# A Hymba layer on one core: the first raw conv weights loaded ahead of the stores of split weights, and the w_up pieces laid over the turned conv input

## The chip, the cores and the metric

One Trainium2 chip, one of its cores. The time is device microseconds of one launch of the whole layer, the median of three runs. Lower is better. The engines are PE (matrix products), DVE and ACT (vector and scalar work), POOL (GpSimd) and SP, which here only issues transfers; the transfers themselves are carried by the core's 16 DMA engines.

## The reference

One layer, on x of 1 x 2048 x 1024 in float32 (2048 positions, width 1024, 8 heads of 64 with 2 key/value heads, a causal window of 128, 512 conv channels, an MLP of 4096). Weights and gains are inputs.

```python
h = rms_norm(x, attn_norm_g)
z = h @ w_in                       # columns: q 512, k 128, v 128, gate_b 512, gate_c 512, xc 512
q, k = rms_norm(q, q_norm_g), rms_norm(k, k_norm_g)
y_attn = swa_sink_attention(q, k, v, sinks)
y_conv = gate_b * short_conv(gate_c * xc, conv_w)      # 3 taps, causal, per channel
y = concat([rms_norm(y_attn, attn_out_g), rms_norm(y_conv, conv_out_g)])
x = x + y @ w_out
hm = rms_norm(x, mlp_norm_g)
x = x + square(relu(hm @ w_up)) @ w_down
```

## The kernel before

**Arithmetic.** Each product of float32 matrices is made as three products of a high and a low part: ACT casts a raw tile to the high part, DVE subtracts it from the raw tile for the low part (this pair is called a split below). PE then multiplies high by high, high by low and low by high (L266 to L268, `mm3`). Weights are split once, in the first chunk, and both parts are stored to DRAM (`keep`, L223), so that later chunks load them ready-made (`weights`, L230, with c above 0).

**Stages.** The 2048 positions are worked in 4 chunks of 512 rows, each in 4 tiles of 128. Of the first chunk, the function `first_chunk` (L476) is ordered by hand: it loads x and the q columns of w_in in 8 pieces k, splits them (`split0`), turns x, scales it (`moved`), multiplies (`product0`, L508), and then does the k and v columns (qkv2, L266 to L268 into pz) and moves the results to z with ACT (L565 for q, L571 for k and v). At k of 3 it issues the raw load of qkv2 and, behind it, the small loads of conv taps and gains (`load_gains(1)`: cw, g_cols, g_y, L465 to L472). Then the mixers of the four chunks run: attention blocks (q and k normalised at L634 to L641, turned by PE at L652, scores at L679), between them the conv's products (pc from the weights wc, px from wx, pb from wb, in pairs of channel tiles j of 0 and 1, `conv_pair`), and the out projection (pout, from w_wo). Then MLP up (u, L1421), in a scheme of seven products p over blocks of 512 by 512 in place of eight, with wop as the split w_up and op_x as the split input; then MLP down (d, L1528).

**Order.** Outside the hand-ordered part a scheduler puts the work of every engine in an order by priorities. `ahead` raises them, and LATER (250) lowers them for the stores of split weights. Each engine runs its instructions in that order, and an instruction that waits holds up all behind it. SP issues the loads and most of the stores; it uses 8 semaphores in turn, so an issue also waits until the transfer eight issues before it has landed.

**Memory.** Tiles are taken from pools by tag; a tag has a number of buffers, used in turn, and a new tile waits until the readers of the old one in the same buffer are done. Raw weights share 2 buffers (tag "raw"), split weights 4 (tag "w", NW, 2 for each weight): w_wb takes the buffers of w_wc. The split w_q takes 4 buffers of "wop" and, for k of 4 to 7, buffers of "at" (`hl0`). Rows of x for the residual are in tag "x1" (4 buffers). When the mixers end, their pool is closed, and MLP up opens one in the same memory (L1094 on). There a memset of one element to the first tile of each tag (L1105) sets the order in which the tags are laid out, and so which old tile lies under which new one. Tag "w" there has 17 buffers for raw pieces of w_up (`wu`, loaded at L411), of 128 x 512.

Lines of the profile that the prediction uses: raw loads of weights L239, raw qkv L547, split stores of qkv2 and of each weight L228, stores of w_q L586, casts and subtractions of a split weight L245 and L246, x1 loads L965, xt_a loads L370; in MLP up the loads of w_up L411, their splits L416 and L417, op_x loads L396 and casts L397, the store of x to x_dram by POOL L913, its reload as xt_m for the last chunk's norm L1219, copies and activations of u by ACT L1176 and L1179.

Of the kernel before, what the change touches and what calls it, by code (L numbers as in the profile page):

```python
# [7 lines left out]
F32 = mybir.dt.float32  # L8
F32R = mybir.dt.float32r
# [7 lines left out]
P = 128  # L17
D = 1024
S = 2048
KD = D // P  # L20
# [82 lines left out]
def hymba_layer(  # L103
# [119 lines left out]
    def keep(hl, name):  # L223
        parts_dram[name] = [dram.tile([P, 2048], F32, name=f"{name}_{i}") for i in range(2)]

        with tc.high_priority(offset=-LATER):
            for d, t in zip(parts_dram[name], hl):
                nc.sync.dma_start(d, t.bitcast(F32))  # L228

    def weights(src_list, c, name, gains=(None,) * 4):  # L230

        if c:
            hl = high_low(c, f"w_{name}{c}")
            for d, t in zip(parts_dram[name], hl):
                nc.sync.dma_start(t.bitcast(F32), d)
            return hl
        raw = raw_part(f"raw_{name}")
        for dst, src in src_list(raw):
            nc.sync.dma_start(dst, src)  # L239
        hl = high_low(c, f"w_{name}")  # L240
        with ahead(7):
            for i, g in enumerate(gains):
                r = slice(i * 512, (i + 1) * 512)
                if g is None:
                    nc.scalar.copy(hl[0][:, r], raw[:, r])  # L245
                    nc.vector.tensor_tensor(hl[1][:, r], raw[:, r], hl[0][:, r].bitcast(F32), op=ALU.subtract)  # L246
                else:
                    nc.scalar.activation(hl[0][:, r], raw[:, r], AF.Copy, scale=g)
                    nc.vector.scalar_tensor_tensor(
                        hl[1][:, r], raw[:, r], g, hl[0][:, r].bitcast(F32), op0=ALU.mult, op1=ALU.subtract  # L250
                    )
        keep(hl, name)
        return hl
# [182 lines left out]
    z0 = [zrow(f"z0_{t}") for t in range(NT)]  # L436
    raw0 = [raw_part(f"raw_q{half}") for half in range(2)]
    hl0 = [wop_pool.tile([P, 2, AW], F32R, tag="wop", name=f"w_q0_{k}", bufs=NWOP) for k in range(NWOP)]
    hl0 += [pool.tile([P, 2, AW], F32R, tag="at", name=f"w_q0_{k}", bufs=NAT) for k in range(NWOP, KD)]
    h = parts(pool, "h", "a0")  # L440


# [15 lines left out]
    def load_gains(part):  # L458
        if not part:
            nc.sync.dma_start(g_qk[:, 0, :], q_norm_g[0].partition_broadcast(P))  # L460
            nc.sync.dma_start(g_qk[:, 1, :], k_norm_g[0].partition_broadcast(P))
            nc.sync.dma_start(sink, sinks[0].partition_broadcast(P))
            return
        for t in range(3):
            nc.sync.dma_start(cw[:, :, t], conv_w[0][t].rearrange("(i p) -> p i", p=P))  # L465
        nc.sync.dma_start(g_cols, mlp_norm_g[0].rearrange("(k p) -> p k", p=P))
        for kv in range(KVH):
            nc.sync.dma_start(
                g_y[kv * DH : (kv + 1) * DH, 0, :],
                attn_out_g[0][kv * GQ * DH : (kv + 1) * GQ * DH].rearrange("(i d) -> d i", d=DH),  # L470
            )
        nc.sync.dma_start(g_y[:, 1, :], conv_out_g[0].rearrange("(i p) -> p i", p=P))  # L472

    def first_chunk(first):

# [66 lines left out]
        for k in range(KD):  # L542
            split0(k)
            moved(k)
            if k == KH - 1:
                raw = raw_part("raw_qkv2")
                nc.sync.dma_start(*cols256(wi, AW)(raw)[0])  # L547
                load_gains(1)
            if k >= KH:
                norm_stats(x0[:, k - KH], f"a0_{k - KH}", rs0[:, k - KH : k - KH + 1])  # L550
            if k + 1 < KD:
                product0(k, [(i, t) for i in range(3) for t in range(NT)])
            else:
                product0(k, [(i, t) for t in range(NT) for i in range(3)])
            if k + 2 < KD:
                turn(k + 2)
        rs0_in = nc.gpsimd.tensor_tensor(rs0_2, rs0, rs0, op=ALU.mult).ins
        hl = high_low(0, "w_qkv2")
        for i in range(4):
            r = slice(i * 512, (i + 1) * 512)  # L560
            nc.scalar.copy(hl[0][:, r], raw[:, r])
            nc.vector.tensor_tensor(hl[1][:, r], raw[:, r], hl[0][:, r].bitcast(F32), op=ALU.subtract)
        w4 = [w.rearrange("p (k c) -> p k c", k=KD) for w in hl]
        for t in range(NT):
            nc.scalar.activation(z0[t][:, :AW], pzs[t], AF.Copy, scale=rs0[:, t : t + 1])  # L565
        for t in range(NT):
# [2 lines left out]
            for k in range(KD):  # L569
                mm3(ps, lambda s, k=k: hk(s, k), lambda s, k=k: w4[s][:, k, :], k == 0, k == KD - 1)  # L570
            z_in.append(nc.scalar.activation(z0[t][:, AW:], ps, AF.Copy, scale=rs0[:, t : t + 1]).ins)  # L571
        return rs0_in, hl

    z_in = []

    with tc.tile_pool(name="first", bufs=1) as first:
        with tc.manual_schedule(engines={ET.PE, ET.Activation, ET.DVE, ET.Pool, ET.SP}):
            rs0_in, w_qkv2 = first_chunk(first)

    keep(w_qkv2, "qkv2")  # L580
    for half in range(2):
        d = dram.tile([2, P, 2048], F32, name=f"q{half}")
        parts_dram[f"q{half}"] = [d[i] for i in range(2)]
        with tc.high_priority(offset=-LATER):
            for k in range(KH):
                nc.sync.dma_start(  # L586
                    d[:, :, k * AW : (k + 1) * AW].rearrange("i p c -> p i c"), hl0[half * KH + k].bitcast(F32)
                )

    with tc.tile_pool(name="mix_small", bufs=1) as mix_small, tc.tile_pool(name="mix", bufs=1) as mix:

# [199 lines left out]
        def conv_pair(c, h, j, yt, ssc):  # L793
# [30 lines left out]
            for i in range(2):  # L824
# [14 lines left out]
                conv.append(y)  # L839
                yield  # L840
            hl = weights(cols256(wi, O_B + j * 256), c, f"wb{j}")
            for i in range(2):
                ct = 2 * j + i
                ps = bank("mm", f"pb_{nm}_{i}")
                yield from group(hl, ps, i)
                y = conv[i]
                with ahead(10):
                    nc.vector.tensor_tensor(y, ps, y, op=ALU.mult)
                    yh = wop_pool.tile([P, 2, CH], F32R, tag="wop", name=f"yt_{nm}_{i}", bufs=NWOP)
                    yt.append(yh)  # L850
                    nc.scalar.copy(yh[:, 0], y)
                    nc.vector.tensor_tensor(yh[:, 1], y, yh[:, 0].bitcast(F32), op=ALU.subtract)
                    if ct == 0:
                        nc.scalar.activation(ssc, y, AF.Square)
                    else:
                        nc.scalar.activation(y, y, AF.Square)
                        nc.vector.tensor_tensor(ssc, ssc, y, op=ALU.add)
                yield
# [96 lines left out]
        def besides(c, before, h, yt, rc, x1, h_next, z_next):  # L955

            yield from before
            ssc = mix.tile([P, CH], F32, tag="ssc", name=f"ssc{c}", bufs=1)
            for j in range(2):
                yield from conv_pair(c, h, j, yt, ssc)  # L960
            for t in range(NT):
                r = (c * NT + t) * P
                xr = row("x1", f"x1_{c}_{t}", NT)
                with nullcontext() if c else tc.issue_after(z_in[-1]):
                    nc.sync.dma_start(xr, xf[r : r + P, :])  # L965
                x1.append(xr)
            out = out_projection(c, 1, yt, rc, x1)
            if c + 1 < NCHUNK:
                h_next += parts(pool, "h", f"h{c + 1}")
                steps = prepare(xf, (c + 1) * CH, g_row[0], h_next, f"a{c + 1}")  # L970
            else:
                steps = prepare_mlp(gain_row(mlp_norm_g, "g_mlp"))
            for i, _ in enumerate(steps):
                yield
                for j in range(STEPS):
                    next(out, None)
                    yield
                    if (i, j) == PC:
                        pc = bank("tr", f"pc{c}")
                        for t in range(NT):  # L980
                            nc.tensor.matmul(
                                pc[:, t : t + 1], ssc[:, t * P : (t + 1) * P], mean, start=True, stop=True
                            )
                        ms = mix_small.tile([P, NT], F32, tag="msc", name=f"ms_c{c}", bufs=1)

                        with tc.high_priority(offset=SOON):
                            if c:
                                nc.vector.tensor_copy(ms, pc[:, :NT])
                                rsqrt(rc, ms)
                            else:  # L990
                                nc.vector.tensor_tensor(ms, pc[:, :NT], rs0_2, op=ALU.mult)
                                rsqrt(rc, ms)
                                nc.gpsimd.tensor_tensor(rc, rc, rs0, op=ALU.mult)
            yield from out
            if c + 1 < NCHUNK:
                yield from project_qkv(c + 1, h_next, z_next)
            else:
                begin_mlp()
# [102 lines left out]
        return pool.tile([P, BW], F32, tag=tag, name=name, bufs=UP_BUFS[tag])  # L1101


    for tag in ("f12", "s1", "s2", "s4", "u4", "f11", "w"):
        nc.gpsimd.memset(piece(tag, f"{tag}_first")[:, :1], 0.0)  # L1105


    class Weights:
# [459 lines left out]
```

## Time and profile before

| what | us |
|---|---|
| median of 3 runs | 1934.71 (1933.54 to 1935.15) |
| the profiled execution | 1934.5 |
| its span, first to last instruction | 1932.8 |
| PE busy | 1913.2 |
| DVE busy | 1204.1 |
| ACT busy | 830.8 |
| POOL busy | 275.9 |
| PE busy in MLP up (L1421), 2688 products | 611.7 |
| PE busy in MLP down (L1528), 2688 products | 609.4 |
| DMA, mean over the span | 214 GB/s |

The span is what lies between the first and the last instruction; the 1.7 us beside it are start and end. Matmuls overlap in the array, so a group's "mean of one" (390 ns in MLP up) is longer than the spacing of two, and spacing is what counts. The granted clock of PE was 0.998 on the mean. Read a row of a timeline as: start, duration, engine, line, operation, what is written from what is read, shapes, how many; the bracket gives the idle time of the engine ahead of it and what ended it. SPq is SP's issue of a transfer; DMA in the chain of waits is from issue to landing.

### The profile page before, as it was taken

Reading aid. Unit: us, or ns where it says so; the run is one execution under the profiler, and the core shown is the slowest. Engines: PE = TensorE matmul, PEld = TensorE weight load, DVE = VectorE, ACT = ScalarE, POOL = GpSimd, SP = SyncE. Lnnn points to the kernel's source line nnn. Section 1 sums busy time; section 2 is a strip of 40 time slices with the busy share of each in tenths; the row PEclk is TensorE's granted clock in tenths of the full one; section 3 lists DMA queues with packets and bytes.
Section 4 is the critical chain, followed back from the end, with each engine's and each line's share of the span. In section 5 each row is a group of like instructions: output and inputs, shape, how many; then the busy total and the mean of one; then the engine's idle time right before and its main releaser. Section 6 shows DMA issues by size and latency. Waiting matters only on the chain.

```text
span 1932.8 us, 24559 instructions
## 1 busy us (share of the span) xinstructions
PE 1913.2 (99%) x8923; PEld 1589.5 (82%) x8923; DVE 1204.1 (62%) x1848; ACT 830.8 (43%) x1565; POOL 275.9 (14%) x474
## 2 busy tenths in 40 slices
PE   8999999999999989999999999999999999999999
PEld 7888888888888778888888888888888888888887
DVE  4886657447456768989877766766534334448541
ACT  5564435335344437444565554554422233232320
POOL 1122212302221112223201110101000000100000
PEclk9999999999999999999999999999999999999999
DMA  9884854464463888777665544537964457766631
GB/s 295 321 306 135 312 211 175 187 249 153 193 267 140 264 282 283 232 235 245 209 233 195 181 162 138 169 124 294 378 211 152 142 164 228 264 228 223 206 135 55
DMA packets 232792, 414.32 MB, mean 214 GB/s; under 512 B 51672, under 2 KB 136160, under 8 KB 219872
## 3 DMA queue, kind: packets, MB, share of 16 engines
q1 hardware_dynamic: 203840, 336.98, 51.8%
q0 software_dynamic: 15424, 51.40, 6.8%
q10 hardware_dynamic: 13408, 24.39, 3.3%
q8 instruction: 70, 1.15, 0.2%
q14 instruction: 50, 0.41, 0.1%
HBM read 286.87 MB, written 125.83 MB: 214 GB/s over the span
## 4 chain that ended last, share of the span: by engine, by line
PE 93%; DMA 2%; DVE 2%; issue 1%; POOL 1%; ACT 1%; SPq 0%; ACTq 0%; POOLq 0%; DVEq 0%
PE d L1528 32%; PE u L1421 31%; PE pout L266 2%; PE pout L268 2%; PE pout L267 2%; PE pz L266 2%; PE pz L267 2%; PE pz L268 2%; PE psc_b L679 2%; PE pc_c L266 2%; PE px_c L266 2%; PE px_c L267 2%; PE pc_c L267 2%; PE pc_c L268 2%; PE px_c L268 2%; PE pb_c L267 1%
## 5 line engine op out<-in xcount | busy, mean ns | idle before, releaser
L1421 PE MATMUL u<-op_x,wop 128*128 128x512 f32 x2688 | 611.7, 390 | 4.6 <-ACT wop L416 4.6
L1528 PE MATMUL d<-op_w,op_f 128*128 128x512 f32 x2688 | 609.4, 389 | 0.0
L1421 PEld LDWEIGHTS u<-op_x,wop 128*128 128x128 f32 x2688 | 505.4, 188 | 110.3 <-ACT wop L416 5.2
L1528 PEld LDWEIGHTS d<-op_w,op_f 128*128 128x128 f32 x2688 | 504.5, 188 | 104.8
L398 DVE TENSOR_TENSOR op_f<-op_f 128x1024 fp32r<-128x1024 f32 x112 | 136.9, 1225 | 234.0 <-ACT op_f L397 233.6
L397 ACT CAST op_f<-op_f 128x1024 fp32r<-128x1024 f32 x112 | 117.5, 1050 | 353.3 <-DMA op_f<-fop 350.2
L416 ACT CAST wop<-wu 128x512 fp32r<-128x512 f32 x156 | 96.2, 620 | 89.9 <-PE u L1421 82.4
L417 DVE TENSOR_TENSOR wop<-wu,wop 128x512 fp32r<-128x512 f32 x156 | 110.6, 710 | 32.6 <-ACT wop L416 17.3
L1157 POOL DMA_DIRECT2D fop<-s x96 | 52.2, 543 | 440.5 <-DVE s L1160 436.3
L1163 DVE TENSOR_TENSOR u<-u,u 128x512 f32<-128x512 f32 x128 | 87.7, 685 | 22.1 <-PE u L1421 22.0
L398 DVE TENSOR_TENSOR op_w<-raw,op_w 128x1024 fp32r<-128x1024 f32 x56 | 68.4, 1222 | 26.3 <-ACT op_w L397 26.2
L397 ACT CAST op_w<-raw 128x1024 fp32r<-128x1024 f32 x56 | 58.8, 1053 | 44.9 <-PE d L1528 22.6
L1169 ACT ACTIVATE u<-u 128x512 f32<-128x512 f32 x64 | 40.5, 632 | 62.9 <-DVE u L1163 61.0
L696 ACT ACTIVATE sc_b<-sc_b,ngm_b 128x128 f32<-128x128 f32 x128 | 49.6, 389 | 25.6 <-DVE ngm_b L693 25.6
L728 POOL TENSOR_SCALAR_AFFINE_SELECT pp_b<-pp_b 128x512 fp32r<-128x512 f32 x60 | 39.8, 675 | 112.8 <-ACT pp_b L721 59.2
L1370 POOL DMA_DIRECT2D wds<-raw x16 | 8.6, 536 | 328.1 <-DVE raw L1368 328.1
L416 ACT CAST wop<-wu_s 128x512 fp32r<-128x512 f32 x64 | 39.6, 620 | 32.2 <-PE u L1421 26.1
L417 DVE TENSOR_TENSOR wop<-wu_s,wop 128x512 fp32r<-128x512 f32 x64 | 45.0, 702 | 12.4 <-ACT wop L416 12.1
L266 PE MATMUL pout<-w_wo,yt_c 128*128 128x512 f32 x128 | 52.5, 410 | 0.0
L268 PE MATMUL pout<-w_wo,yt_c 128*128 128x512 f32 x128 | 52.1, 407 | 0.0
L267 PE MATMUL pout<-w_wo,yt_c 128*128 128x512 f32 x128 | 51.2, 400 | 0.0
L266 PE MATMUL pout<-w_wo,at_b 128*128 128x512 f32 x128 | 50.2, 395 | 0.0
(256 smaller groups left out, 3109.4 us busy)
## 6 DMA issues: line engine op xcount, KB each, us to landing
op_f<-fop SPq DMA_DIRECT2D x112, 512.0 KB, 4.3
raw<-in_w_down_dram SPq DMA_DIRECT2D x72, 512.0 KB, 4.3
wu<-in_w_up_dram SPq DMA_DIRECT2D x128, 256.0 KB, 4.1
w_wo<-wo SPq DMA_DIRECT2D x24, 1024.0 KB, 6.8
fop<-s POOLq DMA_DIRECT2D x96, 256.0 KB, 2.5
fop<-u ACTq DMA_DIRECT2D x64, 256.0 KB, 2.9
op_x<-xop SPq DMA_DIRECT2D x28, 512.0 KB, 6.4
w_q<-q SPq DMA_DIRECT2D x12, 1024.0 KB, 6.2
```

Of the source, the lines that this page charges most:

```text
L266: nc.tensor.matmul(ps, st(0), mv(0), start=first, stop=False)
L267: nc.tensor.matmul(ps, st(0), mv(1), start=False, stop=False)
L268: nc.tensor.matmul(ps, st(1), mv(0), start=False, stop=last)
L397: nc.scalar.copy(op[:, 0], raw)
L398: nc.vector.tensor_tensor(op[:, 1], raw, op[:, 0].bitcast(F32), op=ALU.subtract)
L416: splits.append(nc.scalar.copy(hi, blk).ins)
L417: nc.vector.tensor_tensor(lo, blk, hi.bitcast(F32), op=ALU.subtract)
L696: nc.scalar.activation(sc[:, hd, :], sc[:, hd, :], AF.Exp, bias=ngm[:, hd : hd + 1], accum_out=den[:, hd : hd + 1])
L1157: eng.dma_start(fop_dram[tb][ORDER_DOWN.index(i)][n // 2][:, n % 2], b)
L1163: return nc.vector.tensor_tensor(dst, ps, b, op=ALU.add).ins
L1421: nc.tensor.matmul(pt, wops[i][:, a, k, :], xops[tb, p][k // 2][:, b, k % 2, :], start=p not in GOES_ON and k + j == 0, stop=k + j == NB + ...
L1528: nc.tensor.matmul(ps[tb][j], fs[tb][:, a, k, j * P : (j + 1) * P], w[:, b, k, :], start=first and p not in GOES_ON and k + n == 0, stop=l ...
```

## The change

In the first chunk: the raw load of wc (the first pair of conv weights) moves from the scheduled part into `first_chunk`, at k of 7, and the small gain loads go behind it; the stores of qkv2 and of w_q 0 to 3 are issued at the end of `first_chunk`; the stores of w_q 4 to 7 are written behind the first wb weights, without the lowered priority; the split w_q 4 to 7 lie in rows of x1 in place of "at"; the loads of x for the residual of chunk 0 have no pinned predecessor. In MLP up: the memsets lay the tags out in another order, with two more (st, xt), and w last.

```diff
--- before.py
+++ after.py
@@ -227,6 +227,15 @@
             for d, t in zip(parts_dram[name], hl):
                 nc.sync.dma_start(d, t.bitcast(F32))
 
+    raws = {}
+
+    def load_raw(src_list, name):
+
+        raw = raw_part(f"raw_{name}")
+        for dst, src in src_list(raw):
+            nc.sync.dma_start(dst, src)
+        return raw
+
     def weights(src_list, c, name, gains=(None,) * 4):
 
         if c:
@@ -234,9 +243,7 @@
             for d, t in zip(parts_dram[name], hl):
                 nc.sync.dma_start(t.bitcast(F32), d)
             return hl
-        raw = raw_part(f"raw_{name}")
-        for dst, src in src_list(raw):
-            nc.sync.dma_start(dst, src)
+        raw = raws.pop(name, None) or load_raw(src_list, name)
         hl = high_low(c, f"w_{name}")
         with ahead(7):
             for i, g in enumerate(gains):
@@ -436,7 +443,7 @@
     z0 = [zrow(f"z0_{t}") for t in range(NT)]
     raw0 = [raw_part(f"raw_q{half}") for half in range(2)]
     hl0 = [wop_pool.tile([P, 2, AW], F32R, tag="wop", name=f"w_q0_{k}", bufs=NWOP) for k in range(NWOP)]
-    hl0 += [pool.tile([P, 2, AW], F32R, tag="at", name=f"w_q0_{k}", bufs=NAT) for k in range(NWOP, KD)]
+    hl0 += [row("x1", f"w_q0_{k}", NT, F32R).rearrange("p (i c) -> p i c", i=2) for k in range(NWOP, KD)]
     h = parts(pool, "h", "a0")
 
 
@@ -471,6 +478,14 @@
             )
         nc.sync.dma_start(g_y[:, 1, :], conv_out_g[0].rearrange("(i p) -> p i", p=P))
 
+    def keep_q(half):
+        d = dram.tile([2, P, 2048], F32, name=f"q{half}")
+        parts_dram[f"q{half}"] = [d[i] for i in range(2)]
+        for k in range(KH):
+            nc.sync.dma_start(
+                d[:, :, k * AW : (k + 1) * AW].rearrange("i p c -> p i c"), hl0[half * KH + k].bitcast(F32)
+            )
+
     def first_chunk(first):
 
         x0 = first.tile([P, NT, D], F32, name="x0")
@@ -543,8 +558,9 @@
             split0(k)
             moved(k)
             if k == KH - 1:
-                raw = raw_part("raw_qkv2")
-                nc.sync.dma_start(*cols256(wi, AW)(raw)[0])
+                raw = load_raw(cols256(wi, AW), "qkv2")
+            if k == KD - 1:
+                raws["wc0"] = load_raw(cols256(wi, O_C), "wc0")
                 load_gains(1)
             if k >= KH:
                 norm_stats(x0[:, k - KH], f"a0_{k - KH}", rs0[:, k - KH : k - KH + 1])
@@ -560,6 +576,8 @@
             r = slice(i * 512, (i + 1) * 512)
             nc.scalar.copy(hl[0][:, r], raw[:, r])
             nc.vector.tensor_tensor(hl[1][:, r], raw[:, r], hl[0][:, r].bitcast(F32), op=ALU.subtract)
+        keep(hl, "qkv2")
+        keep_q(0)
         w4 = [w.rearrange("p (k c) -> p k c", k=KD) for w in hl]
         for t in range(NT):
             nc.scalar.activation(z0[t][:, :AW], pzs[t], AF.Copy, scale=rs0[:, t : t + 1])
@@ -569,25 +587,13 @@
             for k in range(KD):
                 mm3(ps, lambda s, k=k: hk(s, k), lambda s, k=k: w4[s][:, k, :], k == 0, k == KD - 1)
             z_in.append(nc.scalar.activation(z0[t][:, AW:], ps, AF.Copy, scale=rs0[:, t : t + 1]).ins)
-        return rs0_in, hl
+        return rs0_in
 
     z_in = []
 
     with tc.tile_pool(name="first", bufs=1) as first:
         with tc.manual_schedule(engines={ET.PE, ET.Activation, ET.DVE, ET.Pool, ET.SP}):
-            rs0_in, w_qkv2 = first_chunk(first)
-
-    keep(w_qkv2, "qkv2")
-    for half in range(2):
-        d = dram.tile([2, P, 2048], F32, name=f"q{half}")
-        parts_dram[f"q{half}"] = [d[i] for i in range(2)]
-        with tc.high_priority(offset=-LATER):
-            for k in range(KH):
-                nc.sync.dma_start(
-                    d[:, :, k * AW : (k + 1) * AW].rearrange("i p c -> p i c"), hl0[half * KH + k].bitcast(F32)
-                )
-
-
+            rs0_in = first_chunk(first)
 
     with tc.tile_pool(name="mix_small", bufs=1) as mix_small, tc.tile_pool(name="mix", bufs=1) as mix:
 
@@ -839,6 +845,8 @@
                 conv.append(y)
                 yield
             hl = weights(cols256(wi, O_B + j * 256), c, f"wb{j}")
+            if not c and not j:
+                keep_q(1)
             for i in range(2):
                 ct = 2 * j + i
                 ps = bank("mm", f"pb_{nm}_{i}")
@@ -961,8 +969,7 @@
             for t in range(NT):
                 r = (c * NT + t) * P
                 xr = row("x1", f"x1_{c}_{t}", NT)
-                with nullcontext() if c else tc.issue_after(z_in[-1]):
-                    nc.sync.dma_start(xr, xf[r : r + P, :])
+                nc.sync.dma_start(xr, xf[r : r + P, :])
                 x1.append(xr)
             out = out_projection(c, 1, yt, rc, x1)
             if c + 1 < NCHUNK:
@@ -1101,8 +1108,10 @@
         return pool.tile([P, BW], F32, tag=tag, name=name, bufs=UP_BUFS[tag])
 
 
-    for tag in ("f12", "s1", "s2", "s4", "u4", "f11", "w"):
+    for tag in ("u2", "f11", "f12", "s1", "s2", "s4", "u4", "st"):
         nc.gpsimd.memset(piece(tag, f"{tag}_first")[:, :1], 0.0)
+    nc.gpsimd.memset(pool.tile([P, D], F32, tag="xt", name="xt_m_first", bufs=2)[:, :1], 0.0)
+    nc.gpsimd.memset(piece("w", "w_first")[:, :1], 0.0)
 
 
     class Weights:
```

How this moves the transfers on SP, first in the first chunk. The rows are issues in SP's order: line, then destination and source. g_attn is a gain row, raw_qkv, raw_wc, raw_wx, raw_wb are raw weights, q the stores of the split w_q, qkv and wc the stores of the split weights, cw, g_cols and g_y the small loads, x_0 and xt_a rows of x. Before, from the store of w_q_0 on:

```order
L586 DMA q_616<-w_q_0_242 128x2x512
L586 DMA q_616<-w_q_1_243 128x2x512
L547 DMA raw_qkv_371<-in_w_in_dram 128x8x256
L465 DMA cw<-in_conv_w_dram 128x4x1 x3
L466 DMA g_cols<-in_mlp_norm_g_dram 128x8x1
L468 DMA g_y<-in_attn_out_g_dram 64x4x1 x2
L472 DMA g_y<-in_conv_out_g_dram 128x4x1
L586 DMA q_621<-w_q_4_246 128x2x512
L586 DMA q_621<-w_q_5_247 128x2x512
L586 DMA q_616<-w_q_2_244 128x2x512
L586 DMA q_621<-w_q_6_248 128x2x512
L239 DMA raw_wc_674<-in_w_in_dram 128x8x256
```

And now, from the same place, the row behind g_attn:

```order
L377 DMA xt_a_0_1425<-in_x_dram 128x1024
L377 DMA xt_a_1_1434<-in_x_dram 128x1024
L236 DMA raw_qkv_371<-in_w_in_dram 128x8x256
L485 DMA q_916<-w_q_4_246 128x2x512
L485 DMA q_916<-w_q_5_247 128x2x512
L485 DMA q_916<-w_q_6_248 128x2x512
L972 DMA x_0_0_1415<-in_x_dram 128x1024
L236 DMA raw_wc_467<-in_w_in_dram 128x8x256
L472 DMA cw<-in_conv_w_dram 128x4x1 x3
L473 DMA g_cols<-in_mlp_norm_g_dram 128x8x1
L475 DMA g_y<-in_attn_out_g_dram 64x4x1 x2
L479 DMA g_y<-in_conv_out_g_dram 128x4x1
```

raw_wc stood behind the small loads and four stores of w_q; it now stands ahead of the small loads, behind two loads of xt_a, three stores of w_q and one x row.

What follows on SP until the last store of the split wc, before:

```order
L586 DMA q_616<-w_q_3_245 128x2x512
L239 DMA raw_wx_764<-in_w_in_dram 128x8x256
L228 DMA qkv_0_612<-w_qkv_0_492 128x2048
L239 DMA raw_wb_905<-in_w_in_dram 128x8x256
L228 DMA qkv_1_613<-w_qkv_1_493 128x2048
L586 DMA q_621<-w_q_7_249 128x2x512
L228 DMA wc_0_686<-w_wc_0_676 128x2048
L228 DMA wc_1_687<-w_wc_1_677 128x2048
```

And now:

```order
L236 DMA raw_wx_759<-in_w_in_dram 128x8x256
L228 DMA qkv_0_504<-w_qkv_0_494 128x2048
L228 DMA qkv_1_505<-w_qkv_1_495 128x2048
L485 DMA q_508<-w_q_0_242 128x2x512
L485 DMA q_508<-w_q_1_243 128x2x512
L485 DMA q_508<-w_q_2_244 128x2x512
L485 DMA q_508<-w_q_3_245 128x2x512
L236 DMA raw_wb_900<-in_w_in_dram 128x8x256
L485 DMA q_916<-w_q_7_249 128x2x512
L228 DMA wc_0_681<-w_wc_0_671 128x2048
L228 DMA wc_1_682<-w_wc_1_672 128x2048
```

raw_wx and the stores of qkv now follow the small loads; the stores of w_q_0 to w_q_3 stand between those of qkv and raw_wb.

The second place is SP at the start of MLP up. wu are raw pieces of w_up (12, 21, 22, 11 name the block), op_x parts of the input, xt_m the reloaded rows of x. Before:

```order
L396 DMA op_x_2_0_6821<-xop_1_77 128x1024
L396 DMA op_x_2_1_6825<-xop_1_77 128x1024
L1219 DMA xt_m_0_7369<-x_dram 128x1024
L396 DMA op_x_6_0_6829<-xop_2_78 128x1024
L396 DMA op_x_6_1_6833<-xop_2_78 128x1024
L411 DMA wu_12_6839<-in_w_up_dram 128x4x128
L411 DMA wu_12_6841<-in_w_up_dram 128x4x128
L411 DMA wu_12_6843<-in_w_up_dram 128x4x128
L411 DMA wu_12_6845<-in_w_up_dram 128x4x128
L411 DMA wu_21_6847<-in_w_up_dram 128x4x128
L411 DMA wu_22_6849<-in_w_up_dram 128x4x128
```

And now:

```order
L403 DMA op_x_2_0_6827<-xop_1_77 128x1024
L403 DMA op_x_2_1_6831<-xop_1_77 128x1024
L403 DMA op_x_6_0_6835<-xop_2_78 128x1024
L403 DMA op_x_6_1_6839<-xop_2_78 128x1024
L418 DMA wu_12_6845<-in_w_up_dram 128x4x128
L418 DMA wu_12_6847<-in_w_up_dram 128x4x128
L418 DMA wu_12_6849<-in_w_up_dram 128x4x128
L418 DMA wu_12_6851<-in_w_up_dram 128x4x128
L418 DMA wu_21_6853<-in_w_up_dram 128x4x128
L418 DMA wu_22_6855<-in_w_up_dram 128x4x128
```

xt_m_0 stood behind the first pair of op_x, ahead of the second pair and of all the wu of the first column group. It now comes 27 rows further down, at the end of these:

```order
L403 DMA op_x_4_1_7146<-xop_6_82 128x1024
L418 DMA wu_21_7168<-in_w_up_dram 128x4x128
L418 DMA wu_22_7170<-in_w_up_dram 128x4x128
L418 DMA wu_11_7172<-in_w_up_dram 128x4x128
L418 DMA wu_11_7236<-in_w_up_dram 128x4x128
L1228 DMA xt_m_0_7375<-x_dram 128x1024
```

The transfers that were behind it keep their order.

## The prediction

> **What bounds the kernel now.** I read the page's first part for the share of each engine, then the list of waits of PE (engine and line, what it waited for, us in total, times, longest), since an edit of load orders can only pay where PE stands still.
>
> ```profile
> PE 1913.2 (99%) x8923; PEld 1589.5 (82%) x8923; DVE 1204.1 (62%) x1848; ACT 830.8 (43%) x1565; POOL 275.9 (14%) x474
> PE u L1421 <- ACT wop L416: 4.6, 1, 4.6
> PE ptq_b L652 <- DVE z L641: 3.0, 1, 3.0
> ```
>
> PE is busy in 1913.2 of 1932.8 us. All its idle time is 19.6 us, and that is the ceiling of any gain by reordering, apart from what a low clock costs after a stop. Two single waits make up 7.6 of it, and the change touches what feeds both.
>
> First stop, in the chain of waits (start us, us, what):
>
> ```profile
> 29.32 9.14 DMA raw_wc<-in_w_in_dram
> 38.47 2.18 ACT w_wc L245 x4
> 46.27 0.70 DVE z L641
> 47.11 0.45 PE ptq_b L652
> ```
>
> The raw conv weights land at 38.46; ACT splits them in four casts, and only then, since ACT runs in order, moves z to SBUF, from which 8.64 us after the first cast (47.11 - 38.47) PE can turn q. ACT's own timeline shows that it had nothing else:
>
> ```profile
> 29.70 2.54 ACT L565 ACTIVATE z<-pz,rs 128x512 f32<-128x512 f32 x4
> 38.47 2.18 ACT L245 CAST w_wc<-raw_wc 128x512 fp32r<-128x512 f32 x4 [6.23 <-DMA raw_wc<-in_w_in_dram]
> ```
>
> ACT was free at 32.24 and waited 6.23 us for a transfer. PE's timeline, and the stretches with the granted clock (the number after the busy times), show what the stop costs:
>
> ```profile
> 47.11 0.45 PE L652 MATMUL ptq_b<-ident,z 128*128 128x128 f32 x1 [3.01 <-DVE z L641]
> 50.23 0.40 PE L268 MATMUL pc_c<-h_a,w_wc 128*128 128x512 f32 x1
> 68.65 0.27 PE L652 MATMUL ptq_b<-ident,z 128*128 128x128 f32 x1
> 69.00 0.27 PE L652 MATMUL ptq_b<-ident,z 128*128 128x128 f32 x1
> 47.00:50.00 3.00, 2.89 (x10) 2.19 (x11) 1.17 (x4) 2.01 (x5) 1.93 (x2) 0.50 1.01 411
> ```
>
> Idle 3.01, then the clock is 0.50: five pairs of one transpose and one matmul take 3.12 us (47.11 to 50.23), where the same pair later takes 0.35 (69.00 - 68.65), 1.75 for five. The stop is worth 3.0 + 1.4 = 4.4 us.
>
> Second stop, the start of MLP up, again in the chain:
>
> ```profile
> 703.02 3.01 DMA x_dram<-x
> 706.05 0.32 SPq L1219
> 707.37 11.13 DMA wu<-in_w_up_dram
> 718.52 0.63 ACT wop L416
> 719.20 20.87 PE u L1421 x84
> ```
>
> SP stands at L1219, the load of xt_m, until the store that POOL issued at 703.02 has landed (706.05). Behind it in SP's order stand the second pair of op_x and all the wu loads, so the wu that PE wants next starts at 707.37 and lands at 718.50, in a heap of transfers. PE:
>
> ```profile
> 709.47 5.15 PE L1421 MATMUL u<-op_x,wop 128*128 128x512 f32 x22
> 719.00:735.00 16.00, 15.80 (x63) 12.92 (x64) 12.43 (x18) 11.02 (x20) 1.64 (x3) 0.89 1.09 362
> 735.00:795.00 60.00, 60.00 (x267) 49.67 (x266) 55.02 (x84) 38.75 (x63) 15.42 (x25) 1.00 0.81 257
> ```
>
> PE is through at 714.62 and starts again at 719.20: 4.6 idle. Then the clock is 0.89 over 16 us: 63 matmuls in 15.80, where at 60.00/267 each they take 14.16, so 1.6 more. The stop is worth 6.2.
>
> **The first chunk's edits.** The load of raw_wc is issued once the last q split has freed its buffer, ahead of the gain loads and of the stores q_2 and q_6. The rows (SP's issues, then DVE's last split of w_q):
>
> ```profile
> 15.04 6.55 SPq L465 DMA_DIRECT2D cw<-in_conv_w_dram  x3
> 25.74 0.60 SPq L472 DMA_DIRECT2D g_y<-in_conv_out_g_dram  x1
> 26.44 2.78 SPq L586 DMA_DIRECT2D q<-w_q  x4
> 32.15 0.67 SPq L239 DMA_DIRECT2D raw_wx<-in_w_in_dram  x1
> 25.05 0.69 DVE L491 TENSOR_TENSOR w_q<-raw_q,w_q 128x512 fp32r<-128x512 f32 x1 [0.79 <-ACT w_q L490]
> ```
>
> The split ends at 25.74, so raw_wc can be issued at about 25.8 in place of 29.32. Its landing is bounded by 1.05 MB at the 336 GB/s of the row for 35 to 40 us below, in an empty queue (28.9), and by the 9.14 us that it took among four stores (34.9). As the new order has a store and one x load, 0.5 MB each, just before it, I take 32.5, about when ACT comes free. PE waits only if the cast starts after 47.11 - 3.01 - 8.64 = 35.46. Both ends lie below that, so the whole 4.4 goes; the cover is the qkv2 products, which with the first conv matmuls keep PE busy to 44.10, and if raw_wc came at 36.5 a microsecond would be left.
>
> What is late in its place: the seven small issues (15.04 to 26.34, 11.3 us of SP's time, with their waits for landings) now stand between raw_wc and raw_wx. So raw_wx is issued near 38.3, 6 us later than before (32.15). Alone at the 398 GB/s below it would land at 41; with what is left of the queue I say 43. ACT comes to its cast some 4.4 us before 48.99, at 44.6. That costs nothing; if it landed later by more than 1.6, ACT's next casts would wait.
>
> After it come qkv_0, qkv_1 and q_0 to q_3 (4.2 MB of stores), and only then raw_wb, q_7, wc_0 and wc_1: raw_wx 1.05, qkv 2.1, q_0 to q_3 2.1, raw_wb 1.05, q_7 0.5 and wc 2.1 (each tile 128 by 2048 f32, or half of it) make 8.9 MB from 38.5 on, before the store wc_1 has landed. The splits of w_wb write over the buffers of w_wc, so they wait for these stores, ACT's for wc_0 and DVE's for wc_1. Behind them on ACT stand the copies of the scores, on DVE the masking and the maximum, and for these PE waits at the next block's scores. The rows (windows with the GB/s last, then ACT, DVE and PE):
>
> ```profile
> 30.00:35.00 5.00, 5.00 (x38) 4.77 (x37) 2.13 (x4) 2.25 (x4) 0.00 (x0) 1.00 1.01 305
> 35.00:40.00 5.00, 5.00 (x44) 5.00 (x43) 0.87 (x2) 1.53 (x3) 0.00 (x0) 1.00 1.00 336
> 40.00:45.00 5.00, 4.11 (x32) 3.63 (x31) 2.71 (x6) 4.03 (x11) 2.18 (x2) 1.00 1.04 398
> 50.00:55.00 5.00, 5.00 (x23) 4.13 (x23) 2.45 (x4) 3.67 (x10) 2.31 (x3) 0.99 1.04 433
> 48.99 0.61 ACT L245 CAST w_wx<-raw_wx 128x512 fp32r<-128x512 f32 x1
> 66.36 2.49 DVE L246 TENSOR_TENSOR w_wb<-raw_wb,w_wb 128x512 fp32r<-128x512 f32 x4
> 81.15 0.29 DVE L662 TENSOR_TENSOR kw<-ptk_b,kw 64x128 fp32r<-64x128 f32 x1
> 82.88 2.08 PE L679 MATMUL psc_b<-kw,qt_b 128*128 128x256 f32 x16
> ```
>
> DVE was done with kw at 81.44, PE came at 82.88: 1.4 us of slack. With PE 4.4 us earlier the splits must start by 66.36 - 4.4 + 1.4 = 63.4. At 398 GB/s wc_1 lands at 60.9 and costs nothing; at 336 it lands at 65.1 and gives back 1.7. Loads and stores are mixed in both rows. Since 40 to 55, the nearest stretch in time and kind, ran at the faster rate, I take 0.5.
>
> The Trainium skill, "DMA: Bandwidth & Descriptors", Specifications, puts the HBM limit of a core at about 358 GB/s, which speaks against the change: 8.9 MB would take 24.9 us, wc_1 would land at 63.4, and the give-back would be just 0.0 with nothing to spare. The 433 above, on traffic that is HBM on one side throughout, does not agree with it as a ceiling.
>
> The other first-chunk edits cost nothing. That hl0[4..7] lie in x1 rows makes x_0_0 wait for PE's use of w_q_4 and for its store, and x_0_1 to x_0_3 go behind wb_1; their reader is the out projection of chunk 0, after the whole of that chunk's attention. Moving xt_a far ahead only fills the queue where q_0 and q_1 stood, 1.05 MB each way, ahead of raw_qkv. Were they more, 1.05 MB at 336 GB/s would be 3.1 us on raw_qkv, which ACT splits just before its row at 29.70.
>
> **The MLP-up edit.** With the pieces w over the turned conv input, long read when MLP up begins, the wu no longer wait for the rows that are freed last, and xt_m, which now does, goes 27 rows down SP's order, behind the rest of the first op_x. So after the first op_x pair, issued at 692.66, SP has before it only waits for landings of transfers issued up to 693.5:
>
> ```profile
> 692.66 0.80 SPq L396 DMA_DIRECT2D op_x<-xop  x2
> 713.70 1.05 ACT L397 CAST op_x<-op_x 128x1024 fp32r<-128x1024 f32 x1 [10.32 <-DMA op_x<-xop]
> 710.72 0.53 POOL L913 DMA_DIRECT2D x_dram<-x  x1 [2.19 <-DVE x L906]
> ```
>
> The second op_x pair and wu_12 are then issued by about 698 rather than 706.46 and 707.37. Even at the 11.13 us of before they land by 709.1, and the casts end 0.63 + 0.04 later, ahead of 714.62. The 6.2 goes.
>
> What is late there: u2, f11 and f12 now lie over x1 rows. ACT's third copy to u2 must wait for the last store of x, issued at 710.72 and, at the 3.01 us of the store above, landed near 713.7. It stands between the casts of the second and third wop of product 2. PE gets to the third 24 matmuls after 714.62, at 0.225 each near 720, and ACT needs 0.6 + 0.6 from 713.7. Slack 5 us; the price if the store took 9 instead of 3 would be 1. The two more memsets on POOL stand behind that last store, where PE has no wait for POOL in the list.
>
> **Sum**, against the profiled execution's 1934.5 (span 1932.8 and 1.7 around it; 0.2 under the median of 1934.71): 1934.5 - 4.4 - 6.2 + 0.5 = 1924.4.
>
> The Trainium skill, "TensorE: Matmul & The Clock Gate", Part 1, lets the clock fall only after an idle window of some 3.4 us. By it the first stop would be too short to lower the clock, the 1.4 would belong to something that stays, and the sum would be 1925.8. The row of 0.50 right behind 3.01 idle disagrees, so the sum stands; the page itself says that the window runs freely.
>
> **Rivals.** First, the first gain is given back: the queue moves the 8.9 MB at 305 GB/s, the 30 to 35 row. wc_1 lands at 67.7, the splits are 4.3 late, and only the second gain remains: 1934.5 - 4.4 - 6.2 + 4.3 = 1928.2. For it: 4.2 MB of stores now go ahead of raw_wb. Against it: 376 and more from 40 to 55.
>
> Second, the change does not do what it says in MLP up: the wu still start with the last store of x, or the copy to u2 blocks ACT. Then only the first gain is left: 1934.5 - 4.4 = 1930.1. For it: POOL's stores at 703 to 711 remain the last thing in that memory. Against it: they bind xt_m and u2 now, not w.
>
> Third, slower. One mechanism: the same queue, held up not by bandwidth but by SP, whose issues each wait for the landing eight issues before. The mean of the span is the nearest row for such stop-and-go traffic:
>
> ```profile
> HBM read 286.87 MB, written 125.83 MB: 214 GB/s over the span
> ```
>
> At 214, wc_1 lands at 80.1, the splits are 16.7 late, and the kernel takes 1923.9 + 16.7 = 1940.6. It decides from a loss of 10.6, landing at 74.0, that is below 251 GB/s. For it: the tiny loads of 2 KB sit in this queue too, and SP's issue waits are real. Against it: ACT and DVE run these splits in order with work that is itself waiting for PE, so part of the lateness would be hidden.
>
> Fourth, neither stop goes, because each is replaced by the next transfer in line at once: 1934.5.
>
> **Numbers.** Forecast 0.62, first rival 0.15, second 0.09, slower 0.11, nothing 0.03. Forecast's own range: give-back 0 to 1.7, a remainder of the second stop up to 1, another 2 us of small idle (19.6 - 7.6 = 12 is left) either way: 1922 to 1927. The range of 8 in 10 goes over the first and second rivals: 1921.8 to 1930.5. A difference under 0.2% (3.9 us) can't be told from none. Faster: 0.62 + 0.15 + 0.09, less 0.02 for the second rival's edge, 0.84; same 0.03 + 0.02 = 0.05; slower 0.11.
>
> **What will show it.** Right: no wait of PE for z L641 near 44, ACT's cast of w_wc starting at 32 to 33.5, clock 1.00 from 40 to 60; wu landed before 712, PE without a gap from 709 to 735 and its clock 1.00 there; PE's idle down from 19.6 to about 12.5. Wrong: a wait of PE for scores between 78 and 100, with DVE's w_wb splits behind the store wc_1 (first and third rivals); ACT idle between casts of wop at 714 to 720 with PE waiting behind (second). Were PE to lose clock in another place, or idle anywhere in the mixers or in MLP down that is new, the sum would be wrong for a reason that I have not named.

## The result, and the profile after

The changed kernel takes 1926.47 us (median of 6 runs, 1925.4 to 1929.62) against 1934.93 of the kernel before (6 runs, 1933.54 to 1938.19). The ratio is 0.9958, with a 95% interval of 0.9946 to 0.9971: faster by 8.1 us by the ratio, between 5.6 and 10.4 (the two medians lie 8.5 apart). Forecast were 1924.4, in a range of 1921.8 to 1930.5. The profiled execution took 1926.5, its span is 1924.7.

First PE's busy time and its list of waits (engine and line, what it waited for, us in total, times, longest), as they were shown of before:

```profile
PE 1912.8 (99%) x8923; PEld 1589.3 (83%) x8923; DVE 1204.5 (63%) x1848; ACT 829.9 (43%) x1565; POOL 273.4 (14%) x477
PE idle L547 <- POOL ident L170: 1.6, 1, 1.6
PE po_b L773 <- POOL pp_b L734: 1.4, 3, 0.9
PE u L1430 <- DVE wop L424: 0.5, 1, 0.5
```

Both stops are gone from the list. Idle time is 1924.7 - 1912.8 = 11.9 us, where it was 19.6. But PE's busy time fell by only 0.4, though the prediction had 3.0 us of lost clock come back with the stops. Something else cost time on PE, and a stretch of its timeline at the very start shows 1.9 us of it. Before, and then after:

```profile
6.43 3.02 PE L508 MATMUL pz<-w_q,h_a 128*128 128x512 f32 x12 [0.29 <-ACT h_a L500]
```

```profile
5.57 1.12 PE L511 MATMUL pt_a<-ident,x 128*128 128x128 f32 x4 [0.24 <-DMA x<-in_x_dram]
7.11 4.88 PE L523 MATMUL pz<-w_q,h_a 128*128 128x512 f32 x12 [0.42 <-ACT h_a L515]
```

The same 12 products take 3.02 us in one and 4.88 in the other, and they begin 0.7 later: 2.5 us lost before anything that the change touched.

The transfers of the first chunk, SP's issues and ACT's casts after:

```profile
28.30 0.37 SPq L236 DMA_DIRECT2D raw_wc<-in_w_in_dram  x1
34.85 0.45 SPq L236 DMA_DIRECT2D raw_wx<-in_w_in_dram  x1
34.67 2.17 ACT L252 CAST w_wc<-raw_wc 128x512 fp32r<-128x512 f32 x4
60.12 2.19 ACT L252 CAST w_wb<-raw_wb 128x512 fp32r<-128x512 f32 x4 [2.01 <-DMA wc<-w_wc]
```

ACT no longer waits for raw_wc; its cast follows straight on other work. It does wait 2.0 us for the store wc_0, which was the price feared, and PE has no idle time from 60 to 118 us. MLP up, on PE and ACT, and a window of it (busy times of PE, PEld, DVE, ACT and POOL, granted clock, DMA share, GB/s):

```profile
706.86 39.38 PE L1430 MATMUL u<-op_x,wop 128*128 128x512 f32 x173
702.59 1.15 ACT L423 CAST wop<-wu 128x512 fp32r<-128x512 f32 x2
714.88 0.59 ACT L1185 COPY u<-u 128x512 f32<-128x512 f32 x1 [11.14 <-DMA x_dram<-x]
718.00:735.00 17.00, 17.00 (x77) 14.08 (x76) 16.96 (x25) 15.14 (x23) 2.17 (x4) 1.00 0.77 289
```

PE runs through without a gap and at the full clock (the 1.00 in the last row, where before had 0.89 from 719), since the first two wop were cast some 8 us before it wanted them. ACT's copy to u2 waited for the last store of x as forecast. That store took from 708.11 to 714.88, 6.8 us rather than 3.0; the transfers, now with the wu among them, moved 377 GB/s in that time.

### The profile page after: what moved, and what is told of

It is laid out like the page before. It is cut to its first block, busy times and chain, and to the rows that moved or that the text cites. A ratio compares the mean times of both kernels' runs of the same rounds, so it can differ in the third digit from the quotient of the medians.

```text
span 1924.7 us, 24566 instructions
## 1 busy us (share of the span) xinstructions
PE 1912.8 (99%) x8923; PEld 1589.3 (83%) x8923; DVE 1204.5 (63%) x1848; ACT 829.9 (43%) x1565; POOL 273.4 (14%) x477
## 4 chain that ended last, share of the span: by engine, by line
PE 90%; DVE 6%; DMA 2%; issue 1%; ACT 1%; POOL 1%; ACTq 0%; SPq 0%; DVEq 0%; POOLq 0%
PE d L1537 32%; PE u L1430 29%; PE pout L273 3%; PE pout L275 3%; PE pout L274 3%; PE pz L273 2%; PE pz L274 2%; PE pz L275 2%; PE pc_c L273 1%; PE pc_c L275 1%; PE pc_c L274 1%; PE psc_b L685 1%; PE pz L523 1%; PE px_c L274 1%; PE px_c L273 1%; PE px_c L275 1%
```

## The experiments

Each kernel was run beside the kernel before on the same chip. In the table, of each profile: the start and length of the first 12 products of q (a start with some 3 us for them is called warm below, one with near 5 cold), PE's wait at 47 us for z, its wait near 121 us for ms_b, the granted clock from 118 to 135 us, and the start of the first po_b after 127 us, which says how far along PE is once the first chunk's effects are through. "-" is a wait under 0.3. The ratio compares the runs of one set and need not be the quotient of the two medians; where they tell different things, the text gives both.

| kernel | first 12 products | at 47 | near 121 | clock | po_b | ratio to before |
|---|---|---|---|---|---|---|
| before | 6.43, 3.02 | 3.01 | - | 1.00 | 131.63 | |
| changed | 7.11, 4.88 | - | - | 1.00 | 129.91 | 0.9958 |
| first chunk alone | 7.39, 3.02 | - | 1.88 | 0.90 | 131.62 | 0.9995 |
| MLP up alone | 6.42, 5.08 | 0.63 | 1.50 | 1.00 | 132.09 | 0.9956 |
| changed, dummy products | 6.57, 3.04 | - | 1.87 | 0.90 | 130.90 | 0.9956 |
| changed, small loads first | 6.42, 5.06 | - | - | 1.00 | 129.12 | 0.9947 |
| changed, wc early | 6.89, 3.04 | - | - | 1.00 | 127.55 | 0.9959 |
| the same, dummy products | 7.25, 3.02 | - | - | 1.00 | 127.90 | 0.9949 |
| before, dummy products | 6.72, 3.03 | 2.58 | - | 1.00 | 131.61 | 1.0002 |
| first chunk alone, wc early | 6.43, 4.69 | - | - | 1.00 | 128.66 | 0.9980 |
| changed, once more | 7.33, 4.64 | - | - | 1.00 | 129.97 | 0.9962 |
| wc early, dummy products, once more | 7.45, 3.00 | - | - | 1.00 | 127.99 | 0.9953 |

**The first chunk's part alone.** The changed kernel with the old loop of memsets:

```diff
-    for tag in ("u2", "f11", "f12", "s1", "s2", "s4", "u4", "st"):
+    for tag in ("f12", "s1", "s2", "s4", "u4", "f11", "w"):
         nc.gpsimd.memset(piece(tag, f"{tag}_first")[:, :1], 0.0)
-    nc.gpsimd.memset(pool.tile([P, D], F32, tag="xt", name="xt_m_first", bufs=2)[:, :1], 0.0)
-    nc.gpsimd.memset(piece("w", "w_first")[:, :1], 0.0)
```

> The changed first chunk, with the memset order of MLP up as it was before. Theory (two stops that add, each its own): the first stop is gone and the second stands, so about 1930.5 us, 4.3 below before; PE waits 4.6 us for ACT's cast of wop at the start of MLP up and its clock falls there. Rival (the first stop's gain is given back later in the mixers, and the whole gain is that of MLP up): 1934 to 1935. On the start of the kernel, where the changed kernel's profile has its first 12 products of q in 4.9 us at half clock and before has them in 3.0 us: if that is chance of the run, the four profiles of this set show either length whatever the kernel; if the change causes it, this one and the gains-first one show 4.9 and the MLP-up one 3.0.

Measured: 1932.93 us (10 runs) against 1933.89 (13 runs), ratio 0.9995, 0.9985 to 1.0006. The rival was right: the part that was worth 4.3 by the prediction gained 1.0, between -1.2 and 2.9. The first stop is gone, and a new one stands at 121 us. PE's timeline, and the window from 118 to 135 (busy times by engine, granted clock, DMA share, GB/s):

```profile
121.17 0.66 PE L301 MATMUL pt_a<-ident,xt_a 128*128 128x128 f32 x4 [1.88 <-DVE ms_b L796]
118.00:135.00 17.00, 14.96 (x75) 11.62 (x73) 14.21 (x25) 12.19 (x34) 5.14 (x9) 0.90 0.72 226
```

The same window of the changed kernel, which had come to this place later, has no stop and the full clock:

```profile
118.00:135.00 17.00, 15.99 (x88) 12.70 (x87) 14.90 (x27) 12.58 (x35) 6.66 (x11) 1.00 0.74 256
```

1.88 idle and a clock of 0.90 over 17 us (1.7 lost) take back 3.6. What the stop waits for, in the chain of waits of the part alone (start us, us, what):

```profile
89.56 0.38 SPq L236
89.98 10.12 DMA wc<-w_wc
100.20 2.50 DVE w_wb L253 x4
...
121.17 0.66 PE pt_a L301 x4
```

It is the mechanism feared for the first pair of conv weights, at the second pair: the splits of w_wb wait for the store wc_1. That store stands behind a raw load of w_out (L236), which waits until DVE has freed its buffer at 89.5. It lands at 100.1, and from there DVE works almost without a pause to 121.

That wc_1 stands behind the load of w_out (raw_wo) is the change's own doing. SP's issues there in the kernel before:

```profile
86.69 0.38 SPq L239 DMA_DIRECT2D raw_wb<-in_w_in_dram  x1
87.12 1.05 SPq L228 DMA_DIRECT2D wc<-w_wc  x2
93.13 0.38 SPq L239 DMA_DIRECT2D raw_wo<-in_w_out_dram  x1
```

And in the changed kernel:

```profile
84.35 0.65 SPq L228 DMA_DIRECT2D wc<-w_wc  x1
89.25 0.38 SPq L236 DMA_DIRECT2D raw_wo<-in_w_out_dram  x1
89.67 0.94 SPq L228 DMA_DIRECT2D wc<-w_wc  x1
```

So PE and DVE came earlier, but wc_1 went out 2 us later than before.

**The MLP-up part alone**, the kernel before with the new loop of memsets (the same diff turned round).

> The first chunk as before, with the changed memset order of MLP up alone. Theory: the second stop of 4.6 us idle and 1.6 us of lost clock goes, a wait of 0.5 us for a split of wop near 838 us comes in its place, so 5.7 below before, about 1929.1; the first stop (3.0 idle, five slow pairs) stands. Rival: only part of it goes (a late start of MLP up just moves the wait), 1931 or more. The start of the kernel: see the run of the first chunk alone.

Measured: 1927.47 us (4 runs), ratio 0.9956, 0.9939 to 0.9972. By the medians that is 6.4 us below before, by the ratio 8.5; the interval holds both the 6.2 of the prediction and the 8.1 of the whole change, so these four runs don't tell whether the part is worth all of the gain. The second stop is gone, as expected; the wait near 838 us did not come. What was not expected is the first stop in this profile, whose first chunk is that of before:

```profile
6.42 5.08 PE L508 MATMUL pz<-w_q,h_a 128*128 128x512 f32 x12
46.76 0.30 PE L652 MATMUL ptq_b<-ident,z 128*128 128x128 f32 x1 [0.63 <-DVE z L641]
```

It has 0.63 idle in place of 3.01, and the clock behind it is full. The start was cold here (5.08), PE came to 46.1 two microseconds later, and the landing of raw_wc had those two to spare. So the start is chance of the run, for both lengths occur with either first chunk; and in the kernel before a cold start and the first stop are not added. The larger sets them: PE goes on near 47 whatever the start was (47.11, 46.76 here, 46.99 with the dummy products below). With no clock lost at 47, PE then came early to the step near 121 and waited there 1.50 (at 123.17), with the first chunk of before.

**Dummy products at the start.**

```diff
-SPIN = (5, 0)
+SPIN = (5, 4)
```

> The changed kernel with 4 dummy products on PE between the first and the second set of turns of x, so that PE does not idle while the second piece of x is on its way. Theory (the 2.5 us lost at the start of the changed kernel's profile are 0.7 of a late transfer and 1.9 of a clock that stayed at half because PE idled 0.66 us in the first 7 us): the first 12 products take 3.0 us, and the kernel is up to 1.9 us faster than the changed one, or no more than 0.5 slower. Rival (the clock's rise at the start goes by a fixed phase and dummy work does not move it): the first 12 products take 3.0 or 4.9 as before, and the time is that of the changed kernel plus up to 0.7.

Measured: 1927.27 us (4 runs), ratio 0.9956, 0.994 to 0.9973. The first 12 products took 3.04 us, as the theory had it, but the time did not fall: PE met the wall at 121 (1.87 idle, clock 0.90), and po_b began at 130.90, a microsecond later than after the changed kernel's cold start. The expectation missed here by leaving out what stands behind the start.

**The small loads put back ahead of raw_wc.**

```diff
                 raw = load_raw(cols256(wi, AW), "qkv2")
+                load_gains(1)
             if k == KD - 1:
                 raws["wc0"] = load_raw(cols256(wi, O_C), "wc0")
-                load_gains(1)
```

> The changed kernel with the seven small loads of taps and gains put back ahead of the stores of w_q and of raw_wc, where the kernel before had them; raw_wc is still issued from the hand-ordered part. Theory (the order on SP is what moved raw_wc): these issues wait for landings until about 26 us, then the x row waits for a store to land, and raw_wc goes out at 30 to 34, lands at 37 to 41, and ACT waits for it again: PE stops 1.5 to 5 us before the first turn of q, with slow clock behind, 1928 to 1932. Rival (taking raw_wc out of the scheduled part is enough): no stop, 1926.5.

Measured: 1925.91 us (4 runs), ratio 0.9947, 0.9929 to 0.9966. The theory missed and its rival was right: no stop, and not 1928 to 1932. raw_wc went out at 28.89, not past 30, since the small loads were done by 25.0:

```profile
28.89 0.62 SPq L236 DMA_DIRECT2D raw_wc<-in_w_in_dram  x1
36.85 2.18 ACT L252 CAST w_wc<-raw_wc 128x512 fp32r<-128x512 f32 x4 [2.58 <-DMA raw_wc<-in_w_in_dram]
```

It landed 2.2 us later than ACT's cast in the changed kernel, and ACT waited for it, yet PE did not: 36.85 and the 8.64 to z give 45.5, and PE, after a cold start, came at 46. Whether a warm start would stop there isn't shown. So the place of the small loads decides little about the first stop. What this kernel showed by chance was another thing: its order on SP has both wc stores of the second pair ahead of the load of w_out, as in the kernel before, and po_b began 0.8 earlier than in the changed kernel.

**The stores wc of the second pair issued early.** This takes that up by itself:

```diff
-        with tc.high_priority(offset=-LATER):
+        with tc.high_priority(offset=-(200 if name == "wc1" else LATER)):
```

> The changed kernel with the stores of the second pair's split wc (wc_0, wc_1) ahead of the x rows and of the raw load of w_out on SP, where the scheduler had put them behind. Theory (the first stop's gain is taken away again near 121 us: DVE's splits of w_wb wait for the store wc_1, which was issued at 89.7 behind a raw load that waits for DVE and landed at 99.9, and DVE's 21 us of work behind them end at 121, so PE, if it comes early, idles 1.9 us there and loses 1.5 of clock): wc_1 is issued near 83 and lands before 96, the wait for ms_b near 120 is under 0.5 us, and the median is 1 to 3 below the changed kernel's 1926.5 in a paired comparison, near 1924.5. Rival (DVE is simply full from 60 to 121 us, and the store only the last that it waits for): the wait near 121 stays above 1 us whenever the start is warm, 1926 to 1927.

Measured: 1925.44 us (5 runs), ratio 0.9959, 0.9945 to 0.9972; the changed kernel has 0.9958 in its own set, so the medians don't show the gain. The profile does. SP's issues and DVE:

```profile
76.34 0.32 SPq L228 DMA_DIRECT2D wc<-w_wc  x1
82.91 0.57 SPq L228 DMA_DIRECT2D wc<-w_wc  x1
93.19 1.88 DVE L253 TENSOR_TENSOR w_wb<-raw_wb,w_wb 128x512 fp32r<-128x512 f32 x3
127.55 0.49 PE L773 MATMUL po_b<-pp_b,vz 128*128 128x512 f32 x1
```

wc_1 goes out 6.8 us earlier, the splits start at 93.2 in place of 100.0, the stop near 121 is gone with a warm start, and po_b begins at 127.55: 4.1 before the kernel before, which is the 4.4 of the prediction's first term, less a later start of 0.5. DVE is not simply full, then.

**The same, with the dummy products.**

> The same with the 4 dummy products at the start, which keep the first 12 products at 3.0 us in place of 3.0 or 5.0. Theory (a cold start and the wall at 121 hide each other; with neither, the first chunk's 4.4 comes through whole): no wait above 0.5 us before 130 but the first for ident, 1922 to 1924, the fastest of all so far. Rival (PE then meets the next late thing, another wall in the first 300 us): a new wait of 1 to 3 us behind 121, and no better than the kernel without the dummy products.

Measured: 1924.27 us (5 runs), ratio 0.9949, 0.9936 to 0.9961. That is the lowest of its set, and just outside the expected 1922 to 1924. No stop near 121, and no new wall: the 0.9 us for pp_b at 132 is in every kernel of the table, and the next wait above 1 us is at 667 us, where the kernel before has the same 1.76:

```profile
666.68 0.63 PE L315 MATMUL pt_m<-ident,xt_m 128*128 128x128 f32 x4 [1.76 <-DVE xt_m L289]
```

**The kernel before with the dummy products** (the same one-line edit).

> The kernel before with the 4 dummy products at the start. Theory (in the kernel before, the landing of raw_wc sets when PE may go on at 47 us, so what the start gains is lost there): the first 12 products take 3.0 us, the first stop is there with at least 2.5 us idle and a low clock behind it, and the time is that of before, ratio 0.999 to 1.001. Rival (start and stop are independent, and a warm start is worth its 2 us): ratio 0.9985 to 0.999.

Measured: 1935.12 us (11 runs) against 1934.26 (15 runs), ratio 1.0002, 0.9994 to 1.0011. A warm start is worth next to nothing in the kernel before (1.2 us at most, by the interval). The stop of 2.58 us stands, and po_b begins at 131.61.

**The first chunk's part with the early wc stores**, MLP up as before (both edits above).

> The changed first chunk with the early stores of the second pair's wc, and MLP up's memset order as before: the part that alone gained nothing, without its wall near 121 us. Theory: no wait near 121, the first chunk's gain arrives, 2 to 4.4 below before (1930 to 1932), ratio 0.998 to 0.9985, where the part alone had 0.9995; the second stop of 4.6 stands. Rival (the first chunk's gain is lost for other reasons): ratio 0.9995 again.

Measured: 1931.21 us (11 runs) against 1935.47 (15 runs), ratio 0.9980, 0.9972 to 0.9989: 3.9 us faster, between 2.1 and 5.4. Alone, without the early stores, the part had 0.9995, in another set on another chip; the two intervals overlap only between 0.9985 and 0.9989. That is the test of the whole account: take the wall at 121 away and the first chunk's part is worth about what the prediction gave it. This profile had a cold start (4.69), and its po_b came 1.1 later than that of the early-store kernel with a warm one: without the wall, the start shows.

**The changed kernel and the fastest one, side by side.**

> The changed kernel once more, beside the next one on the same chip: 1925.4 to 1929.6, and in the profile either a cold start (first 12 products 4.9 to 5.1) without a stop at 121, or a warm start (3.0) with one of 1.5 to 2 us and the clock at 0.9 behind it; po_b near 134 to 135.7 in both cases.

> The fastest kernel so far beside the changed one: 1.5 to 3 us below it, with po_b near 132 and no stop before it.

Measured in one set, 5 runs each: 1927.37 us (1926.91 to 1928.16) and 1925.65 us (1924.98 to 1926.73). The ranges do not overlap; the difference is 1.7, for the early stores and the dummy products together. The po_b of the expectations is a later one than the table's, behind the 0.9 us for pp_b; it began at 134.09 and 132.11, as expected. The changed kernel's profile had a cold start again (4.64 for the 12 products), no stop at 121, and po_b at 129.97. That a warm start of this very kernel stops at 121 was seen only with the dummy products in it and in the part alone.

## Why the prediction was right, and where it was off

The time lay in the range, 2.1 us over the forecast, and the sign and the larger term held. By the medians the two parts alone gained 1.0 and 6.4, so what the forecast had too much lies in the first stop. By its steps:

- **The second stop, 6.2 us.** Right, in place and size. From before to after, PE's start of u moved from 692.7 to 690.1, and the end of the span by 8.1, so 5.5 came from there on, to which a new wait of 0.5 for a split of wop at 838 us has to be added back: 6.0. The part alone gained 6.4 by its medians and 8.5 by its ratio, whose interval takes in 6.2.
- **What would be late there, the copy to u2.** Right in kind. The store took 6.8 us instead of 3.0. The price had been read from a store in an emptier queue (175 GB/s from 703 to 706, against 377 here), which is the likely reason; the slack of 5 shrank to under 1 (the third split was ready at 716.7, PE wanted it near 717.3).
- **raw_wc issued at 25.8, landed at 32.5.** Right. It was issued at 28.30, as soon as DVE's last split of w_q had ended (28.27), which is 25.75 on a clock that starts 2.55 later, and landed 5.1 us after its issue, at 33.4. ACT's cast began at 34.67 without a wait for it.
- **raw_wx at 38.3.** It went out at 34.85. The 11.3 us of the small issues were waits for earlier landings, not work of SP; in their new place the seven took 6 us (28.73 to 34.75). Carrying a row of issues over to another place with its waits was wrong.
- **The first pair's w_wb, give-back 0.5.** ACT waited 2.0 for wc_0. DVE's splits began at 63.58, where the prediction allowed 63.4, and PE had no wait behind them. Nothing was given back there.
- **The first stop, 4.4 us.** Here the forecast failed. "The whole 4.4 goes" was right at 47 us and wrong at the end of the first chunk, for two reasons. The profile's 3.01 idle was one draw: with a cold start it is 0.63, so the median of before did not hold the whole stop. And the search for what would be late next ended at the first pair of conv weights. At the second pair the store wc_1, which the change put behind the load of w_out, lands at 100 whether PE is early or not, and with DVE's work behind it PE can't pass 121. In the kernel before the store landed at 100.1 too and DVE came free at 122.4, just when PE's own product for this step ended, so that PE has no idle time there and the wall can't be seen. With a warm start the part was worth nothing at po_b (131.62 alone against 131.63 before), with a cold one about 2 (129.91 in the changed kernel against 132.09 in the MLP-up run). The chip gave 1.0 for this part alone, and 3.9 once the wall was moved.

The first rival, that the first gain is given back through the w_wb splits behind a store, was right in mechanism and named the wrong pair; its 1928.2 is about as far from the measured 1926.5 as the forecast is. The slower rival did not occur: wc_0 had landed by 60.1.

The Trainium skill, "TensorE: Matmul & The Clock Gate", Part 1, makes the clock fall after an idle window of some 3.4 us, and calls that window free-running and the number of cold matmuls at a start run-variable. The second half agrees with these runs (3.0 to 5.1 us for the same 12 products). The first does not fit as a threshold: 3.01 us idle gave 0.50 in the next 3 us, and 1.88 gave 0.90 over 17, where 1.50 in the MLP-up run and 1.85 in the small-loads run (at 667 us) left 1.00. With 1.85 and 1.88 so far apart in effect, the idle time alone does not decide; what else does isn't shown.

## What to carry to other kernels

A stop on the critical engine takes up whatever lateness lies ahead of it, so its idle time in one profile is one draw, not its worth; look at the start of that same profile before pricing it. When a stop goes, do not end the search at the next user of the moved transfer: follow each later engine that already works without a pause up to the place where the critical engine meets it, since a wall that it reaches just in step shows no idle time. Look too at what else the edit moves in a queue: here the order of two stores 60 us further on changed with it. And a store that frees a buffer is a deadline like a load: keep it ahead of loads that themselves wait for a buffer.

## What was not expected of the hardware

The first 12 products of the same instructions took between 3.0 and 5.1 us in kernels whose order there is the same (3.02, 4.88, 3.02, 5.08, 5.06, 3.04, 4.69 and 4.64 in the eight profiles without dummy products), while the record of the granted clock shows 1.00 for all of this time. That the clock was low there is inferred from the time of one product, 0.25 against 0.41 us. With the four dummy products it was 3.0 in all four profiles. That they are the cause isn't shown by so few, and why a start is slow stays open: 5.08 came with no idle time ahead of the products, 3.02 with 0.87.
